# A ninth ring slot in a mixture-of-experts layer, half of the gate's weights loaded before the last expert's, and a loop body moved from expert 2 to expert 28

## The chip, the core and the metric

The kernel runs on one core of a Trainium2 chip. The metric is the device time of one execution in microseconds (us), lower being better. A core has TensorE (PE; its weight loads are listed as PEld), VectorE (DVE), ScalarE (ACT), GpSimd (POOL) and SyncE (SP), which here only issues transfers. The core's 16 DMA engines move data between the device's memory and SBUF, the memory on chip.

## The reference, cut to what matters

One layer on 512 tokens of width 1024: attention and retention with an output projection, then a mixture of 32 experts of which each token goes to four, then a gate on a per-layer embedding.

```python
x = x + concatenate([y_a, y_b]) @ w_out                 # attention, retention
hn = rmsnorm(x); top4 = top_k(hn @ w_router + b_router, 4)
for each expert e, for its tokens:                      # 32 experts, 4 of them a token
    h = hn @ w_up_gate[e] + b_up_gate[e]                # 1024 -> 2048
    y = act(h) @ w_down[e] + b_down[e]                  # 1024 -> 1024
    x[token] += gate * y
gate = sigmoid(rmsnorm(x) @ w_ple_gate)                 # 1024 x 1024
x = x + (p @ w_ple_proj) * gate
```

## The kernel before

Everything up to the router takes the first 350 us. Then a loop written out for e = 0 to 31 runs the experts, one after the other. The products of an expert are made with its weights as the moving operand, so the time on TensorE is that of streaming 12.6 MB of weights through it. An expert with more than 64 tokens does more: under an `If` on its count it computes 32 further rows (`up32`, `act32`, `down32`). These are called wide here, the others narrow.

**The ring.** Weights come in pieces of 2 MB: pieces 0 to 3 of an expert are its up and gate weights, 4 and 5 its down weights. They go into eight slots of `[128, 4096]` floats, `NRING = 8`. `load(n)` issues the n-th piece on SP's queue (a down piece as two transfers of half its size); n counts six pieces an expert, with one more item in front of expert 28 (`AT_P`: the embedding rows p and their projection, which stay in their slot to the end) and the two halves of `w_ple_gate` behind the last expert. `ring_slot` says which slot each takes: that of the piece eight before it. In the loop, `load(6 * e + 8 + c)` stands behind the last use of piece c of expert e: for c = 0 to 3 after `up` and `up32`, for 4 and 5 at the expert's end. SP waits there until TensorE has read the slot.

**The results of an expert** go to `y_d` in the device's memory (`rows_out`, `rows_out32`, issued by POOL). In experts 28 to 31 `fetch_all(k)`, k = 3 down to 0, gathers a row for each of the 512 tokens back, in four transfers of 512 KB into four tiles `gy0` to `gy3`, and `add_y(k, t)` adds each into `acc` on DVE at the end of the expert; those of k = 0 are added behind the loop.

**Blocks beyond 96.** `later_blocks()` handles experts with more than 96 tokens, in a loop `For_i(0, nb)` under `If(nb > 0)`. It is called at the start of expert 2. With these inputs no instruction of its body is in the trace: every engine jumps over it.

**The tail.** With `in_order`, the order of PE, DVE, ACT and POOL is that of the code. `g_scale`, `g_hi` and `g_lo` scale the gate's weights and split them into two parts, a row block k of 8 at a time; blocks 0 to 3 (`K0`) are in the first half of `w_ple_gate`, 4 to 7 (`K1`) in the second. Then `yparts` splits the last expert's result, `join_last(t)` adds it into `acc` on TensorE and DVE, `z_parts` turns `acc`, and `terms` and `gated` make the gate's product.

Of the kernel before, what the change touches and what calls it, by code (L numbers as in the profile page):

```python
# [19 lines left out]
P = 128  # L20
# [25 lines left out]
def f32(ap):  # L46
    return ap.bitcast(F32)
# [3 lines left out]
def layer_kernel(ctx, tc, a, out, dbg=None, stop=None):  # L51
# [116 lines left out]
    order = (4, 3, 0, 5, 6, 1, 2, 7)  # L168

    AT_P = 6 * E - 24
    ring_slot = list(order)
    for n in range(NRING, 6 * E + 3):
        ring_slot.append(ring_slot[n - NRING + (n - NRING >= AT_P)])
# [4 lines left out]
    def loaded(e, c):  # L180
        n = 6 * e + c
        return n + (n >= AT_P)

    def piece(e, c):
        return ring(loaded(e, c)).rearrange("p (k f) -> p k f", k=2 if c < 4 else 4)

    def ple_views():
        t = ring(AT_P)
        return (t[:, 0:2 * D].rearrange("p (k d) -> p k d", k=2),
                t[:, 2 * D:2 * D + NT * PLE].rearrange("p (t d) -> p t d", t=NT),  # L190
                t[:, 3 * D:4 * D].rearrange("p (k t) -> p k t", k=2))

    def load(n, halves=(0, 1)):

        if n == AT_P:
# [3 lines left out]
            return  # L201
        if n in (6 * E + 1, 6 * E + 2):
            nc.sync.dma_start(ring(n).rearrange("p (k f) -> p k f", k=4),
                              w_pg.rearrange("(h k p) f -> h p k f", h=2, p=P)[n - 6 * E - 1])
        e, c = divmod(n - (n > AT_P), 6)
        if e < E:
            v = ring(n)
            if c < 4:
                src = w_up[e].rearrange("(m p c) f -> m p (c f)", m=4, c=2)[c]
                if len(halves) == 2:  # L210
                    nc.sync.dma_start(v, src)
                else:
                    o = slice(halves[0] * 2048, halves[0] * 2048 + 2048)
                    nc.sync.dma_start(v[:, o], src[:, o])
            else:
                v = v.rearrange("p (i f) -> p i f", i=2)
                src = w_dn[e].rearrange("(m i p c) f -> m p i (c f)", m=2, i=2, c=2)[c - 4]
                for i in halves:
                    nc.sync.dma_start(v[:, i, :], src[:, i, :])
# [325 lines left out]
    def by_rows(t):  # L545
        return t.rearrange("p (k f) -> p k f", k=4)
# [428 lines left out]
    def later_blocks():  # L975
# [3 lines left out]
        with tc.If(nb > 0):  # L979
            with tc.For_i(0, nb):  # L980
# [31 lines left out]
                oh = m1.tile([P, S], F32R, name="ooh", tag="gy2")  # L1012
# [8 lines left out]
                def rows_of(src, mul, add, per, i):  # L1021

                    fi = m1.tile([P, 1], F32, name=f"ofi{i}", tag="ofi", bufs=2)
                    ii = m1.tile([P, 1], I32, name=f"oii{i}", tag="oii", bufs=2)
                    nc.vector.tensor_scalar(fi, slot, float(per), float(add), op0=ALU.mult, op1=ALU.add)
                    nc.vector.scalar_tensor_tensor(fi, eid, float(mul), fi, op0=ALU.mult, op1=ALU.add)
                    nc.vector.tensor_copy(ii, fi)
                    w = m1.tile([P, D], F32, name=f"ow{i}", tag=f"gy{i % 2}")
# [18 lines left out]
                yy = m1.tile([P, D], F32R, name="oy", tag="gy3")  # L1047
                for h in range(2):
                    pt = dbank(f"opy{h}")
                    hs = slice(h * 512, (h + 1) * 512)  # L1050
                    for k in range(4):
                        nc.tensor.transpose(pt[0:B, k * P:(k + 1) * P], yTo[:, 4 * h + k, :], ident)
                    nc.scalar.activation(yy[0:B, hs], pt[0:B, :], AF.Copy)
                    nc.vector.tensor_tensor(yy[B:2 * B, hs], pt[0:B, :], f32(yy[0:B, hs]), op=ALU.subtract)
                for t in range(NT):
                    nc.vector.scalar_tensor_tensor(key, gates[:, t, 0, :], 1.0, one, op0=ALU.mult, op1=ALU.mult,
                                                   accum_out=st[:, 2:3])
                    for h in range(2):
                        pc = dbank(f"opc{t}{h}")
                        nc.tensor.matmul(pc, oh[:, t * P:(t + 1) * P], yy[:, h * 512:(h + 1) * 512], start=True, stop=True)  # L1060
# [133 lines left out]

    def join_last32():

        ys = []
        for i, tag in enumerate(("gy0", "gy1")):
            ys.append(m1.tile([P, D], F32R, name=f"yq{i}", tag=tag))
# [200 lines left out]
    with in_order:  # L1400
        K0, K1 = (0, 1, 3, 2), (4, 6, 5, 7)
        g_scale(3)
        g_scale(5)
        g_scale(7)
        for t in range(NT):
            add_y(0, t)
        for k in (0, 1, 3, 2):
            g_hi(k)
            g_lo(k)
        yparts = [m1.tile([P, 512], F32R, name=f"yl{i}", tag=("y", "gl")[i]) for i in range(2)]  # L1410
        nc.scalar.activation(yparts[0], y64, AF.Copy)
        nc.vector.tensor_tensor(yparts[1], y64, f32(yparts[0]), op=ALU.subtract)
# [67 lines left out]
```

## Time and profile before

| | before |
|---|---|
| median of three runs | 1502.23 us (1500.53 to 1503.43) |
| the profiled execution's own time | 1501.09 us |
| its span, first to last instruction | 1499.3 us |
| mean granted clock of TensorE, as a share of the full 2.4 GHz | 0.979 |
| TensorE busy | 1359.1 us (91% of the span) |
| DVE, ACT, POOL busy | 451.9, 293.4, 184.1 us |
| moved by DMA | 474.79 MB, 317 GB/s over the span |

The expert loop lies from 349.6 to 1426 us. In it both TensorE and the DMA engines are nearly always busy, so the share of the whole span says little; what counts is which of the two the other waits for, stretch by stretch.

### The profile page before, as it was taken

The page shows a single profiled execution, that of the slowest core. Times are in us where ns is not written, and L with a number is a line of the kernel's source. Part 1 is how long each engine was busy: PE and PEld are TensorE (multiplying, and loading weights), DVE is VectorE, ACT ScalarE, POOL GpSimd, SP SyncE. Part 2 cuts the span into 40 slices and gives each one's busy share as a digit, 9 for nine tenths or more (in the row PEclk, how much of TensorE's full clock was granted, in tenths as well). Part 3 has the DMA queues.
Part 4 walks back from the last instruction along what each step waited for, and adds up shares of the span by engine and source line. Part 5 has one row for each costly group of instructions (what it writes and reads, how often), then busy time and mean ns, then how long its engine had stood idle before and what let it go on. Part 6 is the DMA issues. An engine that isn't in the chain of part 4 may idle for free. (4 is left out here: it accounts for less than half of the span.)

```text
span 1499.3 us, 21638 instructions
## 1 busy us (share of the span) xinstructions
PE 1359.1 (91%) x8629; PEld 657.3 (44%) x8629; DVE 451.9 (30%) x1033; ACT 293.4 (20%) x564; POOL 184.1 (12%) x268
## 2 busy tenths in 40 slices
PE   8999999997979999999989899879999988989868
PEld 7776775563334334334323333423333333333246
DVE  4657596555111121112211111211111121123353
ACT  5645674341000000000000000000000000101043
POOL 3132000010110110110100011000111100212140
PEclk9999999998999999999999999989999999999989
DMA  7203604265979999999999999999999999999921
GB/s 283 85 29 87 155 2 168 69 250 220 362 316 389 407 391 404 410 414 408 410 395 412 404 408 412 412 409 409 407 388 377 375 414 405 407 405 407 417 89 57
DMA packets 65526, 474.79 MB, mean 317 GB/s; under 512 B 9484, under 2 KB 10032, under 8 KB 32400
## 3 DMA queue, kind: packets, MB, share of 16 engines
q1 hardware_dynamic: 54192, 441.69, 73.9%
q0 software_dynamic: 11200, 31.22, 5.9%
q8 instruction: 96, 1.57, 0.4%
q14 instruction: 38, 0.31, 0.1%
HBM read 454.40 MB, written 18.48 MB: 315 GB/s over the span
## 5 line engine op out<-in xcount | busy, mean ns | idle before, releaser
L1148 PE MATMUL yb<-ring,hT 128*64 128x512 f32 x1024 | 244.5, 610 | 34.9 <-DVE hT L1141 26.6
L1090 PE MATMUL glu<-ring,xT 128*64 128x512 f32 x1024 | 252.8, 610 | 20.9 <-DMA ring<-in_w_up_gate_dram 20.8
L1090 PE MATMUL lin<-ring,xT 128*64 128x512 f32 x1024 | 244.2, 592 | 0.0
L1126 DVE TENSOR_SCALAR gl<-glu 128x512 f32<-128x512 f32 x32 | 22.1, 692 | 511.0 <-PE glu L1090 511.0
L1090 PEld LDWEIGHTS glu<-ring,xT 128*64 128x64 f32 x1024 | 83.0, 140 | 153.3 <-issue 112.0
L1090 PEld LDWEIGHTS lin<-ring,xT 128*64 128x64 f32 x1024 | 84.0, 138 | 138.5 <-issue 136.1
L1148 PEld LDWEIGHTS yb<-ring,hT 128*64 128x64 f32 x1024 | 65.7, 137 | 151.6 <-issue 100.9
L890 POOL DMA_INDIRECT xg<-hn_d,idx x32 | 31.1, 971 | 783.4 <-DVE idx L889 441.8
L1104 PE MATMUL u<-ring,xT 128*32 128x256 f32 x2048 | 113.6, 379 | 0.6 <-issue 0.6
L1127 ACT ACTIVATE sg<-gl 128x512 f32<-128x512 f32 x32 | 20.1, 629 | 431.1 <-DVE gl L1126 425.6
L1104 PEld LDWEIGHTS u<-ring,xT 128*32 128x32 f32 x2048 | 63.2, 110 | 46.6 <-issue 1.0
L1161 PE MATMUL yc<-ring,hv 128*32 128x256 f32 x1024 | 58.6, 381 | 8.3 <-DVE hv L1157 8.3
L1172 ACT COPY y<-yb 128x512 f32<-128x512 f32 x31 | 18.1, 585 | 228.9 <-PE yb L1148 228.9
L907 ACT COPY xT<-px 128x384 f32<-128x384 f32 x64 | 27.7, 482 | 155.7 <-PE px L906 155.6
L1161 PEld LDWEIGHTS yc<-ring,hv 128*32 128x32 f32 x1024 | 31.7, 110 | 31.3 <-DVE hv L1157 12.1
L906 PE MATMUL px<-ident,xg 96*128 96x96 f32 x256 | 29.2, 259 | 14.0 <-PEq L1297 7.3
L1174 POOL DMA_DIRECT2D y_d<-y x62 | 33.7, 548 | 63.8 <-ACTq L1317 34.6
L1168 POOL DMA_DIRECT2D y_d<-yv x64 | 31.6, 500 | 54.7 <-ACT yv L1166 48.6
L906 PEld LDWEIGHTS px<-ident,xg 96*128 96x128 f32 x256 | 23.4, 146 | 33.6 <-issue 26.3
L1386 PE MATMUL o<-gh,z 128*128 128x512 f32 x128 | 37.1, 398 | 0.2 <-ACT z L1343 0.2
L886 DVE SCALAR_TENSOR_TENSOR scr<-rk,slot,iot 96x512 bf16<-96x512 f32 x32 | 23.9, 747 | 41.0 <-PE rk L880 40.9
L1223 DVE SCALAR_TENSOR_TENSOR acc<-gy,gk,acc 128x1024 f32<-128x1024 f32 x16 | 20.4, 1284 | 41.2 <-DMA gy<-y_d,yidx 41.0
(960 smaller groups left out, 1701.2 us busy)
## 6 DMA issues: line engine op xcount, KB each, us to landing
ring<-in_w_up_gate_dram SPq DMA_DIRECT2D x127, 2048.0 KB, 17.8
ring<-in_w_down_dram SPq DMA_DIRECT2D x128, 1024.0 KB, 24.9
ring<-in_w_in_dram SPq DMA_DIRECT2D x12, 1024.0 KB, 6.4
y_d<-y POOLq DMA_DIRECT2D x62, 128.0 KB, 9.6
ring<-in_w_out_dram SPq DMA_DIRECT2D x4, 1024.0 KB, 5.9
ring<-in_w_ple_gate_dram SPq DMA_DIRECT2D x2, 2048.0 KB, 29.8
y_d<-none SPq DMA_DIRECT2D x2, 1984.0 KB, 12.3
ring<-in_x_dram SPq DMA_DIRECT2D x4, 512.0 KB, 5.4
```

The costliest lines, as they stand in the source:

```text
L886: nc.vector.scalar_tensor_tensor(scr[0:n], rk[0:n], slots[0:n], iot[0:n], op0=ALU.is_equal, op1=ALU.mult, accum_out=idf[0:n])
L890: nc.gpsimd.indirect_dma_start(out=xg[0:n], out_offset=None, in_=hn_d, in_offset=bass.IndirectOffsetOnAxis(ap=idx[0:n, :1], axis=0))
L906: nc.tensor.transpose(pv[:, k, :], xg[0:n, (4 * h + k) * P:(4 * h + k + 1) * P], ident[0:n, 0:n])
L907: nc.scalar.copy(xT[:, 4 * h:4 * h + 4, 0:n], pv)
L1090: nc.tensor.matmul(o[two(j)], xTs[e][:, 2 * m + c, 0:64], w[:, c, f:f + 512], start=False, stop=m == 3 and c == 1)
L1104: nc.tensor.matmul(u32[four(q), g * 256:(g + 1) * 256], xTs[e][:, 2 * m + c, 64:C], w[:, c, f:f + 256], start=False, stop=m == 3 and c == ...
L1126: nc.vector.tensor_scalar(gl, glu, LIMIT, None, op0=ALU.min)
L1148: nc.tensor.matmul(y64[two(j)], hT[:, fc, :], w[:, fc % 4, j * 512:(j + 1) * 512], start=fc == 0, stop=fc == KD - 1)
L1161: nc.tensor.matmul(y32[four(q), 0:256], hT[:, fc % 2, fc // 2, :], w[:, fc % 4, q * 256:(q + 1) * 256], start=fc == 0, stop=fc == KD - 1, ...
L1168: nc.gpsimd.dma_start(y_d[e * C + 64:(e + 1) * C, q * 256:(q + 1) * 256], y[four(q)])
L1174: nc.gpsimd.dma_start(y_d[e * C:e * C + 64, j * 512:(j + 1) * 512], y[two(j)])
L1386: nc.tensor.matmul(banks[t, h], (zh, zl, zh)[i][:, k, ts], (g_h, g_h, g_l)[i][k // 4][:, k % 4, hs], start=first, stop=last)
```

## The change

1. A ninth slot, index `NRING`, is allocated in the memory that `gy0` to `gy3` take later (one tag `gy`, one tile of the four together). It is loaded once before the loop, and takes its turn in the ring until expert 28 needs its memory for the fetched rows: the pieces of experts 28 and 29 skip it, and it is not used again.
2. `items` lists what is loaded in order, and the first half of `w_ple_gate` ("g0") now stands in front of expert 31's pieces; the second ("g1") stays last. A line of slots replaces the fixed distance of eight: each slot gets the next item as it comes free, and `load_behind(e, c)` loads what follows piece c of expert e.
3. `later_blocks()` is called at expert 28 rather than 2, since its body uses the memory of the fetched rows.
4. In the tail, `g_hi` and `g_lo` of blocks 0 to 3 stand ahead of `g_scale(5)`, `g_scale(7)` and `add_y(0, t)`.

```diff
+    items = [(e, c) for e in range(E) for c in range(6)]
+    items.insert(items.index((E - 4, 0)), "p")
+    items.insert(items.index((E - 1, 0)), "g0")
+    items.append("g1")
+    ring_slot, follows, line = [], {}, [(i, None) for i in order]
+    for n, it in enumerate(items):
+        i, before_it = line.pop(0)
+        if i == NRING and (it == "p" or it[0] in (E - 4, E - 3)):
+            i, before_it = line.pop(0)
+        ring_slot.append(i)
+        if before_it is not None:
+            follows[before_it] = n
+        if it not in ("p", "g0"):
+            line.append((i, n))
+        if n == NRING - 1:
+            line.insert(0, (NRING, None))
...
+    def load_behind(e, c):
+        if nth[e, c] in follows:
+            load(follows[nth[e, c]])
...
+    fresh(NRING, "ring8", pool=m1, tag="gy")
+    load(NRING)
+
     def fetch_all(k):
+        gy = m1.tile([P, NT, D], F32, name=f"gy{k}", tag="gy")
         for t in range(NT):
-            fetch_y(k, t, m1.tile([P, D], F32, name=f"gy{k}{t}", tag=f"gy{t}"))
+            fetch_y(k, t, gy[:, t, :])
     for e in range(E):
-        if e == 2:
+        if e == E - 4:
             later_blocks()
...
         for c in range(4):
-            load(6 * e + 8 + c)
+            load_behind(e, c)
...
         g_scale(3)
+        for k in (0, 1, 3, 2):
+            g_hi(k)
+            g_lo(k)
         g_scale(5)
         g_scale(7)
         for t in range(NT):
             add_y(0, t)
-        for k in (0, 1, 3, 2):
-            g_hi(k)
-            g_lo(k)
```

The rest of the diff gives the body of `later_blocks` other buffers. The new lines shift the code by 13 to 17 lines.

**SP, ahead of the loop and through expert 0.** A row is a line of the code and what is loaded into which slot; `ring_2236` is slot 4, `ring_2594` slot 3, `ring_2595` slot 0, `ring_2601` slot 5, `ring_2602` slot 6, `ring_3035` to `ring_3037` slots 1, 2 and 7. Before:

```order
L211 DMA ring_3037<-in_w_up_gate_dram 128x4096
L1210 TENSOR_LOAD cnts
L1297 COMPARE_AND_BRANCH
L1297 UNCONDITIONAL_BRANCH x2
L211 DMA ring_2236<-in_w_up_gate_dram 128x4096
L1309 COMPARE_AND_BRANCH
L1309 UNCONDITIONAL_BRANCH x2
L211 DMA ring_2594<-in_w_up_gate_dram 128x4096
L1317 COMPARE_AND_BRANCH
L1317 UNCONDITIONAL_BRANCH x2
L219 DMA ring_2595<-in_w_down_dram 128x2048 x2
```

Now, with `ring_3179` the ninth slot:

```order
L224 DMA ring_3037<-in_w_up_gate_dram 128x4096
L224 DMA ring_3179<-in_w_up_gate_dram 128x4096
L1223 TENSOR_LOAD cnts
L1314 COMPARE_AND_BRANCH
L1314 UNCONDITIONAL_BRANCH x2
L224 DMA ring_2236<-in_w_up_gate_dram 128x4096
L1326 COMPARE_AND_BRANCH
L1326 UNCONDITIONAL_BRANCH x2
L232 DMA ring_2594<-in_w_down_dram 128x2048 x2
L1334 COMPARE_AND_BRANCH
L1334 UNCONDITIONAL_BRANCH x2
L232 DMA ring_2595<-in_w_down_dram 128x2048 x2
```

Piece 2 of expert 1, which waited for slot 4 and so for expert 0's first piece, goes into the new slot ahead of the loop; from there on every slot that comes free takes the piece after the one that it took before.

**SP, the loads that stand in expert 30's stretch and the last one.** Before:

```order
L211 DMA ring_3036<-in_w_up_gate_dram 128x4096
L211 DMA ring_3037<-in_w_up_gate_dram 128x4096
L1309 COMPARE_AND_BRANCH
L1309 UNCONDITIONAL_BRANCH x2
L1317 COMPARE_AND_BRANCH
L1317 UNCONDITIONAL_BRANCH x2
L211 DMA ring_2594<-in_w_up_gate_dram 128x4096
L219 DMA ring_2595<-in_w_down_dram 128x2048 x2
L219 DMA ring_2601<-in_w_down_dram 128x2048 x2
L203 DMA ring_2602<-in_w_ple_gate_dram 128x4x1024
```

Now:

```order
L216 DMA ring_2601<-in_w_ple_gate_dram 128x4x1024
L1326 COMPARE_AND_BRANCH
L1326 UNCONDITIONAL_BRANCH x2
L1334 COMPARE_AND_BRANCH
L1334 UNCONDITIONAL_BRANCH x2
L224 DMA ring_2602<-in_w_up_gate_dram 128x4096
L224 DMA ring_3035<-in_w_up_gate_dram 128x4096
L224 DMA ring_3037<-in_w_up_gate_dram 128x4096
L224 DMA ring_2236<-in_w_up_gate_dram 128x4096
L232 DMA ring_2594<-in_w_down_dram 128x2048 x2
```

The first half of the gate's weights stood behind all six pieces of expert 31 and stands ahead of them now; each of the six comes one place later.

**DVE, from the last expert's second `hT` copy (L1141, now L1154) to the split of its result (L1412, now L1429).** `gl` is what `g_lo` writes, `acc<-gy` is `add_y`. Before:

```order
L1141 COPY hT_11201<-ph31b 128x2x2x64
L1309 COMPARE_AND_BRANCH
...
L1309 UNCONDITIONAL_BRANCH x2
L1223 SCALAR_TENSOR_TENSOR acc<-gy_11186,gk,acc 128x1024
L1223 SCALAR_TENSOR_TENSOR acc<-gy_11188,gk,acc 128x1024
L1223 SCALAR_TENSOR_TENSOR acc<-gy_11190,gk,acc 128x1024
L1223 SCALAR_TENSOR_TENSOR acc<-gy_11192,gk,acc 128x1024
L1365 SCALAR_TENSOR_TENSOR gl_11364<-ring_2602,pcol,gh_11362 128x1024 x3
L1412 TENSOR_TENSOR yl_11383<-yb_11197,yl_11382 128x512
```

Now:

```order
L1154 COPY hT_11168<-ph31b 128x2x2x64
L1326 COMPARE_AND_BRANCH
...
L1326 UNCONDITIONAL_BRANCH x2
L1382 SCALAR_TENSOR_TENSOR gl_11331<-ring_2601,pcol,gh_11329 128x1024 x3
L1236 SCALAR_TENSOR_TENSOR acc<-gy_11156,gk,acc 128x1024 x4
L1429 TENSOR_TENSOR yl_11350<-yb_11164,yl_11349 128x512
```

The three `g_lo` have changed places with the four `add_y`.

## Rows read from the trace of the kernel before

**Rows 1.** The page's 40 slices of 37.5 us: GB/s that the DMA engines moved.

```profile
GB/s 283 85 29 87 155 2 168 69 250 220 362 316 389 407 391 404 410 414 408 410 395 412 404 408 412 412 409 409 407 388 377 375 414 405 407 405 407 417 89 57
```

**Rows 2.** Stretches: us, busy time by engine, granted clock, DMA share, GB/s.

```profile
360.00:371.50 11.50, 11.41 (x109) 4.64 (x113) 4.22 (x9) 0.63 (x1) 0.00 (x0) 1.00 0.12 27
...
440.00:452.00 12.00, 11.30 (x58) 4.80 (x54) 2.80 (x6) 1.49 (x3) 0.00 (x0) 1.00 0.21 64
...
560.00:1098.00 538.00, 489.17 (x3437) 193.93 (x3434) 89.42 (x216) 40.18 (x81) 49.84 (x83) 0.99 1.01 408
...
1098.00:1185.00 87.00, 81.64 (x680) 31.99 (x678) 16.86 (x40) 7.21 (x15) 8.01 (x14) 1.00 0.95 379
...
425.00:434.00 9.00, 2.67 (x50) 1.48 (x40) 0.00 (x0) 0.37 (x1) 1.98 (x4) 0.83 1.05 391
```

**Rows 3.** TensorE in order of time: starts of experts 2, 23, 24 and 25.

```profile
433.73 0.67 PE L1084 MATMUL glu<-bst,bsel 96*64 96x512 bf16 x2 [6.33 <-PEq L979]
...
1127.33 0.41 PE L1084 MATMUL glu<-bst,bsel 96*64 96x512 bf16 x2
...
1164.23 0.41 PE L1084 MATMUL glu<-bst,bsel 96*64 96x512 bf16 x2
...
1190.34 0.43 PE L1084 MATMUL glu<-bst,bsel 96*64 96x512 bf16 x2 [0.53 <-PEq L1317]
```

**Rows 4.** TensorE in order of time: waits for weights, experts 13, 20, 29 and 31.

```profile
786.09 3.50 PE L1090 MATMUL glu<-ring,xT 128*64 128x512 f32 x8 [3.47 <-DMA ring<-in_w_up_gate_dram]
...
1027.33 1.94 PE L1090 MATMUL glu<-ring,xT 128*64 128x512 f32 x8 [1.16 <-DMA ring<-in_w_up_gate_dram]
...
1335.41 3.62 PE L1090 MATMUL glu<-ring,xT 128*64 128x512 f32 x8 [2.79 <-DMA ring<-in_w_up_gate_dram]
...
1409.30 1.94 PE L1090 MATMUL glu<-ring,xT 128*64 128x512 f32 x8 [1.14 <-DMA ring<-in_w_up_gate_dram]
```

**Rows 5.** Granted clock and TensorE's work after two idle stretches, same columns as rows 2.

```profile
430.90:437.70 6.80, 3.97 (x12) 1.87 (x14) 0.00 (x0) 0.00 (x0) 0.00 (x0) 0.50 1.04 429
...
1438.90:1444.60 5.70, 4.96 (x18) 3.19 (x19) 3.12 (x5) 1.19 (x2) 4.90 (x2) 0.50 0.00 0
```

**Rows 6.** Ahead of the loop: DVE's last work on the router's tiles; SP's first issue in the loop.

```profile
357.34 0.25 DVE L824 SCALAR_TENSOR_TENSOR hit<-vts,mv,gz 128x31 f32<-128x31 f32 x1
...
369.74 2.06 SPq L211 DMA_DIRECT2D ring<-in_w_up_gate_dram  x2
```

**Rows 7.** TensorE's starts of experts 28 to 31; SP's first issue behind expert 28's up weights.

```profile
1285.90 0.41 PE L1084 MATMUL glu<-bst,bsel 96*64 96x512 bf16 x2
1317.61 0.43 PE L1084 MATMUL glu<-bst,bsel 96*64 96x512 bf16 x2 [0.55 <-PEq L1317]
...
1364.11 0.41 PE L1084 MATMUL glu<-bst,bsel 96*64 96x512 bf16 x2
...
1393.42 0.43 PE L1084 MATMUL glu<-bst,bsel 96*64 96x512 bf16 x2 [0.54 <-PEq L1317]
...
1305.98 1.58 SPq L211 DMA_DIRECT2D ring<-in_w_up_gate_dram  x3
```

**Rows 8.** The tail in order of time, DVE, TensorE and ACT.

```profile
1420.59 0.42 DVE L1141 COPY hT<-ph31b 128x256 f32<-128x256 f32 x1 [3.88 <-PE ph31b L1140]
1421.07 5.37 PE L1148 MATMUL yb<-ring,hT 128*64 128x512 f32 x24 [0.52 <-DVEq L1309]
...
1430.67 1.28 DVE L1223 SCALAR_TENSOR_TENSOR acc<-gy,gk,acc 128x1024 f32<-128x1024 f32 x1 [1.43 <-DMA gy<-y_d,yidx]
1431.37 2.19 ACT L1355 ACTIVATE gh<-ring,pcol 128x1024 fp32r<-128x1024 f32 x2 [18.68 <-DMA ring<-in_w_ple_gate_dram]
1432.56 2.64 DVE L1365 SCALAR_TENSOR_TENSOR gl<-ring,pcol,gh 128x1024 fp32r<-128x1024 f32 x2 [0.61 <-ACT gh L1355]
1438.03 0.68 DVE L1412 TENSOR_TENSOR yl<-yb,yl 128x512 fp32r<-128x512 f32 x1
1438.92 1.31 PE L1187 MATMUL pc<-yl,oh 64*128 64x512 f32 x4 [12.48 <-DVEq L1413]
```

More of the change, by code (lines that the diff above doesn't have):

```diff
@@ L168, in layer_kernel @@
     order = (4, 3, 0, 5, 6, 1, 2, 7)
[L172 to L175, printed above, removed]
+    items = [(e, c) for e in range(E) for c in range(6)]
+    items.insert(items.index((E - 4, 0)), "p")
+    items.insert(items.index((E - 1, 0)), "g0")
+    items.append("g1")
+    nth = {it: n for n, it in enumerate(items)}
+    ring_slot, follows, line = [], {}, [(i, None) for i in order]
[10 more added lines that the diff above has]
+            line.insert(0, (NRING, None))
     def ring(n):
         return slots[ring_slot[n]]
-    def loaded(e, c):
-        n = 6 * e + c
-        return n + (n >= AT_P)
     def piece(e, c):
-        return ring(loaded(e, c)).rearrange("p (k f) -> p k f", k=2 if c < 4 else 4)
+        return ring(nth[e, c]).rearrange("p (k f) -> p k f", k=2 if c < 4 else 4)
+    def load_behind(e, c):
+        if nth[e, c] in follows:
+            load(follows[nth[e, c]])
     def ple_views():
-        t = ring(AT_P)
+        t = ring(nth["p"])
         return (t[:, 0:2 * D].rearrange("p (k d) -> p k d", k=2),
@@ L200, in load @@
             nc.sync.dma_start(wpp, w_pp.rearrange("(k p) d -> p k d", p=P))
[L201 to L202 removed]
+        elif items[n] in ("g0", "g1"):
             nc.sync.dma_start(ring(n).rearrange("p (k f) -> p k f", k=4),
[L204 to L206 removed]
+                              w_pg.rearrange("(h k p) f -> h p k f", h=2, p=P)[int(items[n][1])])
+        else:
+            e, c = items[n]
             v = ring(n)
@@ L1011, in later_blocks @@
                 nc.tensor.matmul(rk, esel, rankT, start=True, stop=True)
-                oh = m1.tile([P, S], F32R, name="ooh", tag="gy2")
+                big = m1.tile([P, 4, D], F32, name="obig", tag="gy")
+                oh = m1.tile([P, S], F32R, name="ooh", tag="y")
                 nc.vector.tensor_scalar(oh, rk, sl, None, op0=ALU.is_equal)
@@ L1027, in rows_of @@
                     nc.vector.tensor_copy(ii, fi)
-                    w = m1.tile([P, D], F32, name=f"ow{i}", tag=f"gy{i % 2}")
+                    w = big[:, i % 4, :]
                     nc.gpsimd.indirect_dma_start(out=w, out_offset=None, in_=src,
@@ L1046, in later_blocks @@
                     nc.scalar.copy(yTo[:, 4 * i:4 * i + 4, :], chunks(yTb[i], B))
-                yy = m1.tile([P, D], F32R, name="oy", tag="gy3")
+                yy = [m1.tile([P, 512], F32R, name=f"oy{h}", tag=("h", "sg")[h]) for h in range(2)]
                 for h in range(2):
                     pt = dbank(f"opy{h}")
-                    hs = slice(h * 512, (h + 1) * 512)
                     for k in range(4):
                         nc.tensor.transpose(pt[0:B, k * P:(k + 1) * P], yTo[:, 4 * h + k, :], ident)
-                    nc.scalar.activation(yy[0:B, hs], pt[0:B, :], AF.Copy)
-                    nc.vector.tensor_tensor(yy[B:2 * B, hs], pt[0:B, :], f32(yy[0:B, hs]), op=ALU.subtract)
+                    nc.scalar.activation(yy[h][0:B], pt[0:B, :], AF.Copy)
+                    nc.vector.tensor_tensor(yy[h][B:2 * B], pt[0:B, :], f32(yy[h][0:B]), op=ALU.subtract)
                 for t in range(NT):
@@ L1059, in later_blocks @@
                         pc = dbank(f"opc{t}{h}")
-                        nc.tensor.matmul(pc, oh[:, t * P:(t + 1) * P], yy[:, h * 512:(h + 1) * 512], start=True, stop=True)
+                        nc.tensor.matmul(pc, oh[:, t * P:(t + 1) * P], yy[h], start=True, stop=True)
                         o = acc[:, t, h * 512:(h + 1) * 512]
@@ L1195, in join_last32 @@
     def join_last32():
-        ys = []
-        for i, tag in enumerate(("gy0", "gy1")):
-            ys.append(m1.tile([P, D], F32R, name=f"yq{i}", tag=tag))
+        yq = m1.tile([P, 2, D], F32R, name="yq", tag="gy")
+        ys = [yq[:, i, :] for i in range(2)]
+        for i in range(2):
             nc.vector.tensor_scalar(ys[i].rearrange("p (a f) -> p a f", f=512), oh, 0.0, None, op0=ALU.mult)
@@ L1320, in layer_kernel @@
         for c in range(4, 6):
-            load(6 * e + 8 + c)
+            load_behind(e, c)
         if k < TOPK:
@@ L1324, in layer_kernel @@
                 add_y(k, t)
-    w_g = [by_rows(ring(6 * E + 1 + i)) for i in range(2)]
-    used = [ring_slot[n] for n in (loaded(E - 1, 4), loaded(E - 1, 5), 6 * E + 1, 6 * E + 2, AT_P)]
+    w_g = [by_rows(ring(nth[f"g{i}"])) for i in range(2)]
+    used = [ring_slot[n] for n in (nth[E - 1, 4], nth[E - 1, 5], nth["g0"], nth["g1"], nth["p"])]
     free = [i for i in range(NRING) if i not in used]
```

2 lines of the change are left out of this document (1 added, 1 removed).

## The prediction

> **What bounds the kernel now.** I read the slices first. From the sixteenth on (562 us) nearly every one moves 404 to 417 GB/s [rows 1], and over 560 to 1098 us the DMA share is 1.01 [rows 2]: the engines are full. TensorE is busy nine tenths of the same time, so both look like the bound, and the waits have to decide. In the list of what TensorE waited for, the stops for weights lie in two stretches, experts 12 to 20 and 27 to 31; four of them are in [rows 4]. An expert that waits for nothing takes 26.1 us when narrow (1164.23 to 1190.34) and 36.9 us when wide (1127.33 to 1164.23) [rows 3]. The stream needs, per piece: from the wait at 786.09 (expert 13, piece 1) to that at 1027.33 (expert 20, piece 3) 44 pieces came in 241.2 us, 5.48 us each with all other transfers, or 32.9 us an expert [rows 4]. About half of the experts are wide, so TensorE would need 31.5 us on average: the stream is the slower of the two, and the ring only decides how much of the stream's time is lost before it becomes the bound. From 1335.41 (expert 29, piece 3) to 1409.30 (expert 31, piece 3) it is 12 pieces in 73.9 us, 6.16 us each, since gathered rows share the engines [rows 4].
>
> So what I price is **idle time of the DMA engines inside the loop**; it moves the end one for one, as long as TensorE still catches up with the stream afterwards. There are three such stretches of size. Share 0.12 over 11.5 us after 360: 10.1 us. Share 0.21 over 12 us after 440: 9.5 us. Share 0.95 against 1.01 over 87 us after 1098 (the three wide experts 21 to 23, where TensorE is slower and the ring is full): 5.2 us [rows 2].
>
> **The tail** is read from the end of the chain of waits, which is TensorE from 1438.92 on. It had finished the last expert at 1426.4 (1421.07 + 5.37) and then sat 12.48 us [rows 8]. What it waited for is a sequence on DVE: the last `add_y` begins at 1430.67, `g_lo` from 1432.56 waits for ACT's `g_hi`, which waited 18.68 us for the gate's weights until 1431.37, and the split of the result (`yl`) is done at 1438.7 [rows 8].
>
> **The change, part by part.**
>
> *Jump moved away from expert 2.* Experts 1 and 2 should meet without a gap, but TensorE sits 6.33 us at the branch over the body, L979 [rows 3], and then works 3.97 us at half clock [rows 5], which loses 2.0: 8.3 us. At that point no weights are waited for, so on TensorE alone this would be absorbed later. But the loads behind expert 2 are issued only when it has used its pieces, and meanwhile the engines run dry: 9.5 us after 440. With TensorE 8.3 us earlier the idle shrinks by 8.3. **-8.3 us** for everything behind it.
>
> *Ninth slot, ahead of the loop.* Its load waits for what used that memory; DVE's last work on the router's tiles ends at 357.6, and SP's first issue in the loop is at 369.74 [rows 6], after which transfers start at about 371.5. The idle stretch has 10.1 us of room, and a piece of 2.1 MB takes 5.0 us even at 417 GB/s [rows 1], so it fits. From there each release of a slot issues the piece after the one it issued before: the stream is one piece ahead at the same instant and its later idle is the same. Where TensorE waits for it (experts 12 to 20) a piece is worth 5.48 us. **-5.5 us**; the lower bound is 0, if the lead were lost before expert 12. Here the Trainium skill (page "DMA: Bandwidth & Descriptors", section Specifications) gives about 358 GB/s as a core's share of the memory; by that an estimate of a piece is 5.9 us. The rows' 408 GB/s over 538 us go beyond it, so the measurement decides, and the sum would differ by 0.4.
>
> *Ninth slot, again at experts 21 to 24.* Behind expert 20 both TensorE and the stream are 13.8 us early. In the 5.2 us of idle that follow the ring is full; one more slot lets the stream go on for up to one piece of 5.0 us. **-5.0 us** (bounds 0 and 5.2).
>
> *Slot retired, jump at expert 28.* From expert 26 on the ring is eight slots again, and TensorE now loses the 8.3 us ahead of expert 28. Where is it then? Expert 24 starts at 1164.23 - 13.8 = 1150.4; three narrow and a wide expert (78.3 + 36.9), 1 us of waits and the jump give 1274.9 for expert 28, against 1285.90 [rows 7]. Its first issue comes 20.1 us after its start (1305.98 - 1285.90), at 1295.0. Had the stream run through, expert 29's piece 0, the last one issued by then, would land at 1335.41 less three pieces (18.5) less 18.8, at 1298.1. So the queue holds 3 us at that moment, which about covers the time from issue to first bytes. Between 0 and 6 us of idle (6 if the jump costs twice as much), I take **+2 us**. The stream is then 16.8 us early.
>
> The jump bears on a rule that speaks against this part: the Trainium skill (page "Runtime: NRT & Kernel Launch", section Instruction fetch mechanics) says that a taken branch to code outside the window forces a DMA fetch of the target before work goes on. At expert 2 the share was 1.05 while TensorE sat there [rows 2], so the 6.33 us were already paid with full engines; I keep the price.
>
> *First half of the gate ahead of expert 31.* Each of its six pieces lands one place later, 6.16 us; the lower bound is 5.0, a bare piece. Piece 3 is used at 1409.30 - 16.8 + 6.2 = 1398.7, 10.6 us earlier than before. TensorE is there in time: from 1274.9 on, experts 28 to 30 take 31.7, 42.0 (46.5 less the wait of 2.79 and 1.7 of half clock) and 29.3 us [rows 4, 7], so expert 31 starts at 1377.9.
>
> *Tail.* The `hT` copy that ended at 1421.0 ends at 1410.4, and TensorE ends at 1415.8. `g_hi` is done by then, so DVE goes on with three `g_lo` (1.32 each, two of them are the 2.64 [rows 8]) to 1414.4, four `add_y` (1.28 each) to 1419.5, and `yl` to 1420.2; TensorE goes on at **1420.4**, 18.5 us earlier. The last row to be added began at 1430.67, 37.3 us after expert 30's end (1393.42); from 1377.9 that is 1415.2, before DVE comes to it. The second half of the gate lands with the end of the stream, about 1416, 20 us before its products.
>
> *Clock.* Before, 4.96 us of TensorE's work behind 1438.90 ran at half clock [rows 5], losing 2.5 us. The stop is now 4.6 us instead of 12.5; behind the 3.47 us stop at 786.09 eight products still took 3.50 us instead of 1.94 [rows 4]. I take **-1 us** of the possible 2.5.
>
> *Free:* reading four rows into one tile makes the first gather of an expert wait for all four additions of the one before. They would end 2 us before the gather's other wait, the landing of the rows just written. If that cover went, each us would go into `add_y` of k = 0, which has 4 us of slack.
>
> **Sum:** -18.5 - 1.0 = -19.5 us on the profiled execution's 1501.09, 1481.6; that execution is 1.1 us under the median of the three, so I say **1482 us** for the median.
>
> **Rivals.**
>
> *Queue dry at expert 28.* For it: 3 us of queue, and a slot fewer. If the idle were 8.3, the whole of the jump, the stream is 10.5 early: 1488. Against: the work above.
>
> *More gain.* No idle at 28, a place in the queue worth 5.0, no half clock behind the tail: 2 + 1.2 + 1.5 more, 1477.
>
> *The lead is worth nothing* because slots come free late anyhow, and only the jump's 8.3 less 2 counts: piece 3 of expert 31 is used at 1409.2, the tail starts 8.0 early: 1493. Against: the engines' idle is plain in the rows.
>
> *Slower.* The jump at expert 28 stalls TensorE much longer than at expert 2. Each us beyond the 8.3 and the 3 in the queue is idle of the stream. It ends slower than before only when the stop at expert 28 passes 6.3 + 21.5 = 28 us; at 32 us the time is 1506. The rows show no stop at a branch over 6.33. (The Trainium skill's page on the runtime, named above, sets no bound to such a fetch.)
>
> *No change:* gains by the lead lost, and the gate's place (+6.2) paid with nothing but the tail's order to win: piece 3 at 1409.30 + 6.2, minus 8.3 and plus 8.3 for the jump, start of the tail at 1437.3: 1500.
>
> **Chances.** My forecast 0.62 (its own range 1478 to 1487), queue dry 0.14, more gain 0.10, lead worthless 0.05, no change 0.04, slower 0.05. The range that leaves out no more than 2 in 10 goes from 1475 to 1491. 0.2% (3 us) is about what this kernel's measurement can tell; faster by more has 0.91, within it 0.04, slower 0.05.
>
> **What would show it.** Right: no gap of 6 us ahead of expert 2 and one ahead of expert 28; a DMA share near 1 instead of 0.95 over the wide experts 21 to 23; waits for weights among experts 12 to 20 later and fewer; expert 31 waiting for its up weights by 2 us or more; TensorE's stop before `pc` about 5 us instead of 12.5. Wrong: a DMA share well under 1 between 1270 and 1320; a stop at expert 28 beyond 8 us; `add_y` of k = 0 waiting for its rows.

## The result, and the profile after

The changed kernel takes **1485.93 us** (median of 4 runs, 1485.12 to 1488.94) against 1502.26 before: a ratio of 0.9896, 95% interval 0.9881 to 0.9911. The profiled execution takes 1485.39 us with a span of 1483.5, so from profile to profile it is 15.7 us faster where 19.5 were forecast. Lines have moved by 13 to 17: L1097 is the start of an expert (L1084 before), L1103 its up products, L992 the branch over the later blocks' body, L1236 `add_y`, L1382 `g_lo`, L1200 `pc`.

Stretches of the changed kernel: us, busy time by engine, granted clock, DMA share, GB/s. The first four answer to those of [rows 2], the fourth 14 us earlier, since TensorE is that much ahead; the last two lie around expert 28's first issue.

```profile
360.00:371.50 11.50, 11.50 (x113) 4.65 (x117) 4.05 (x8) 0.63 (x1) 0.00 (x0) 1.00 0.56 215
425.00:434.00 9.00, 9.00 (x78) 3.44 (x70) 0.00 (x0) 0.37 (x1) 1.98 (x4) 1.00 1.01 360
440.00:452.00 12.00, 10.32 (x51) 3.58 (x49) 4.41 (x11) 1.49 (x3) 0.96 (x1) 1.00 0.88 341
...
1084.00:1171.00 87.00, 80.44 (x670) 31.68 (x668) 16.54 (x39) 7.31 (x15) 8.02 (x14) 0.98 0.97 392
1270.00:1320.00 50.00, 40.15 (x209) 15.55 (x203) 9.49 (x15) 4.91 (x11) 7.87 (x11) 0.93 0.91 350
...
1292.00:1298.00 6.00, 6.00 (x23) 2.15 (x23) 0.00 (x0) 1.17 (x2) 0.00 (x0) 1.00 0.91 366
1298.00:1304.00 6.00, 5.09 (x28) 1.90 (x24) 3.03 (x7) 1.49 (x3) 0.00 (x0) 1.00 0.32 73
```

The hole at 440 has all but closed (share 0.21 to 0.88) and that at 360 by about half (0.12 to 0.56: about the one piece more), and TensorE works through 425 to 434 where it sat. A new hole has opened at 1298: with 1.01 as full, 0.6 + 4.1 us of idle in the two slices, about 5 us with the next one (0.97 over 1304 to 1310).

TensorE in order of time, and SP's first issue behind expert 28's up weights, changed kernel (start, length, work, and in brackets the stop ahead of it and what ended it): the starts of experts 21, 28 and 31, two stops inside experts 24 and 26, and expert 31's waits.

```profile
1039.21 0.41 PE L1097 MATMUL glu<-bst,bsel 96*64 96x512 bf16 x2
...
1166.62 1.35 PE L919 MATMUL px<-ident,xg 96*128 96x96 f32 x8 [2.35 <-PEq L1314]
...
1222.44 0.85 PE L919 MATMUL px<-ident,xg 96*128 96x96 f32 x8 [1.48 <-DVE h L1147]
...
1279.65 0.67 PE L1097 MATMUL glu<-bst,bsel 96*64 96x512 bf16 x2 [7.17 <-PEq L992]
...
1301.95 1.56 SPq L224 DMA_DIRECT2D ring<-in_w_up_gate_dram  x3
...
1383.60 0.43 PE L1097 MATMUL glu<-bst,bsel 96*64 96x512 bf16 x2 [0.54 <-PEq L1334]
...
1386.82 1.94 PE L1103 MATMUL glu<-ring,xT 128*64 128x512 f32 x8 [2.57 <-DMA ring<-in_w_up_gate_dram]
1392.45 1.94 PE L1103 MATMUL glu<-ring,xT 128*64 128x512 f32 x8 [1.97 <-DMA ring<-in_w_up_gate_dram]
```

Expert 28 starts at 1279.65, 6.25 us earlier than in [rows 7], and SP issues the first load behind its up weights at 1301.95, not at the 1295.0 of the forecast. That is where the new hole comes from.

The tail of the changed kernel in order of time, VectorE, TensorE and ACT, which answers to [rows 8].

```profile
1412.98 0.42 DVE L1154 COPY hT<-ph31b 128x256 f32<-128x256 f32 x1 [2.40 <-PE ph31b L1153]
1413.83 3.68 DVE L1382 SCALAR_TENSOR_TENSOR gl<-ring,pcol,gh 128x1024 fp32r<-128x1024 f32 x3 [0.42 <-DVEq L1326]
1417.42 4.87 DVE L1236 SCALAR_TENSOR_TENSOR acc<-gy,gk,acc 128x1024 f32<-128x1024 f32 x4
1422.20 0.69 DVE L1429 TENSOR_TENSOR yl<-yb,yl 128x512 fp32r<-128x512 f32 x1
...
1413.46 5.68 PE L1161 MATMUL yb<-ring,hT 128*64 128x512 f32 x24 [0.52 <-DVEq L1326]
1423.09 1.31 PE L1200 MATMUL pc<-yl,oh 64*128 64x512 f32 x4 [3.95 <-DVEq L1430]
...
1407.01 2.19 ACT L1372 ACTIVATE gh<-ring,pcol 128x1024 fp32r<-128x1024 f32 x2 [0.40 <-PEq L1314]
```

VectorE goes from the copy to the split of the result without a wait, in the order forecast; TensorE's stop is 3.95 us instead of 12.48, and the tail starts at 1423.09 instead of 1420.4.

### The profile page after: what moved, and what is told of

Read it like the earlier page. It is cut to its first block, busy times and chain, and to the rows that moved or that the text cites. A ratio compares the mean times of both kernels' runs of the same rounds, so it can differ in the third digit from the quotient of the medians.

```text
span 1483.5 us, 21634 instructions
## 1 busy us (share of the span) xinstructions
PE 1353.6 (91%) x8629; PEld 652.0 (44%) x8629; DVE 451.4 (30%) x1033; ACT 293.3 (20%) x564; POOL 182.4 (12%) x268
## 5 line engine op out<-in xcount | busy, mean ns | idle before, releaser
L1103 PE MATMUL glu<-ring,xT 128*64 128x512 f32 x1024 | 247.6, 599 | 16.3 <-DMA ring<-in_w_up_gate_dram 16.3
L1103 PE MATMUL lin<-ring,xT 128*64 128x512 f32 x1024 | 245.5, 594 | 0.0
L1103 PEld LDWEIGHTS glu<-ring,xT 128*64 128x64 f32 x1024 | 81.9, 138 | 145.5 <-issue 115.8
L1103 PEld LDWEIGHTS lin<-ring,xT 128*64 128x64 f32 x1024 | 83.0, 137 | 139.5 <-issue 139.5
L903 POOL DMA_INDIRECT xg<-hn_d,idx x32 | 30.5, 954 | 781.3 <-DVE idx L902 469.0
L1140 ACT ACTIVATE sg<-gl 128x512 f32<-128x512 f32 x32 | 20.1, 629 | 408.8 <-DVE gl L1139 408.8
L1141 DVE TENSOR_TENSOR gl<-gl,sg 128x512 f32<-128x512 f32 x32 | 22.2, 692 | 24.4 <-ACT sg L1140 23.7
```

The lines of the kernel that those rows point to most:

```text
L903: nc.gpsimd.indirect_dma_start(out=xg[0:n], out_offset=None, in_=hn_d, in_offset=bass.IndirectOffsetOnAxis(ap=idx[0:n, :1], axis=0))
L1103: nc.tensor.matmul(o[two(j)], xTs[e][:, 2 * m + c, 0:64], w[:, c, f:f + 512], start=False, stop=m == 3 and c == 1)
L1141: nc.vector.tensor_tensor(gl, gl, sg, op=ALU.mult)
```

## The experiments

My theory (A): the end follows the stream of weights; the body's place at expert 2 and the ninth slot ahead of the loop are worth their full price, but at expert 28 TensorE comes late, the DMA queue runs dry for about 5 us and hands most of the lead of experts 21 to 24 back. The rivals: the jump costs the same wherever it stands; the slot's lead is worth nothing; the gate's place, not the stream, made the gain.

Each ratio is to the kernel before on the same chip (1502.49 us for the first four runs, 1500.68 for the next four, 1500.97 for the last four).

| run | median us | ratio to before, 95% interval |
|---|---|---|
| e1_jump28_alone | 1495.58 | 0.996, 0.9947 to 0.9973 |
| e2_after_nojump | 1481.51 | 0.9858, 0.9844 to 0.9872 |
| e3_before_nojump | 1494.93 | 0.9949, 0.9936 to 0.9962 |
| e4_jump31 | 1493.76 | 0.9948, 0.9936 to 0.9961 |
| e5_eight_slots | 1494.27 | 0.9956, 0.9943 to 0.997 |
| e6_slot_till_20 | 1486.74 | 0.9903, 0.9888 to 0.9918 |
| e7_gate_last | 1487.84 | 0.9915, 0.9901 to 0.9928 |
| e8_old_tail | 1486.98 | 0.991, 0.9895 to 0.9925 |
| e9_jump13 | 1480.75 | 0.9866, 0.9851 to 0.9881 |
| e10_jump13_lo_later | 1477.89 | 0.9846, 0.9832 to 0.9859 |
| e11_lo_later | 1485.77 | 0.9905, 0.989 to 0.992 |
| e12_ones_early | 1477.27 | 0.9842, 0.9828 to 0.9855 |

**The body's place** (four runs). The kernel before with the body moved:

```diff
-        if e == 2:
+        if e == E - 4:
             later_blocks()
```

> The kernel before with one edit: the later blocks' body stands ahead of expert 28 instead of expert 2. Theory A (the jump at expert 2 held the stream of weights up, at expert 28 the queue of eight slots hides it): the stream is 8.3 us earlier behind expert 2. Expert 29's piece 0, due about 1316.9 in the kernel before, would come at 1308.6, after the first issue behind the jump (1305.98 - 8.3 + 7.2 = 1304.9), so nothing is given back: 1502.2 - 8.3 = 1494 us. Theory B (the jump costs the same wherever it stands): 1502 us. Theory C (the DMA queue runs dry at expert 28 in this kernel too): 1497 to 1499 us.

The kernel before without the call:

```diff
-        if e == 2:
-            later_blocks()
```

> The kernel before without the later blocks' body; it leaves out the tokens of an expert beyond 96, of which these inputs have none. Theory A (the jump at expert 2, its 6.33 us and 2 us of half clock, puts the stream back one for one): 1502.2 - 8.3 = 1494 us, and as long as with the body at expert 28. Theory B (the ring takes the jump in, since the stream is the bound later): 1502 us.

The changed kernel without it (`if e == E - 4: later_blocks()` taken out):

> The changed kernel without the later blocks' body, so without its jump; it leaves out the tokens of an expert beyond 96, of which these inputs have none. Theory A (the 7.17 us jump ahead of expert 28 lets the DMA queue run dry for about 5 us, and the end follows the stream): expert 28 starts 7.2 us earlier, its first issue comes at about 1294.8, before expert 29's piece 0 lands (1296.24), the stop of the stream at 1292 to 1302 is gone, and the time is 1486 - 5 = 1481 us. Theory B (the jump is hidden at expert 28): 1486 us. Theory C (all 7.2 us of it are on the path): 1479 us or less.

Before gains 7.6 us without the body (1502.49 to 1494.93) and 6.9 us with it at expert 28; the two intervals overlap, so in that kernel expert 28 hides the jump but for 0 to 2 us. The changed kernel gains 4.4 us without it by medians, 5.7 by the ratios. Theory A holds in the second and third of these runs; in the first, 1495.58 lies between A's 1494 and C's 1497, and its trace has about 1 us of idle (share 0.82 over 1306 to 1312). The slice at 1298 of the changed kernel without the jump, and SP's first issue there:

```profile
1298.00:1304.00 6.00, 4.63 (x26) 1.92 (x27) 2.32 (x7) 0.86 (x2) 0.00 (x0) 1.00 0.97 364
...
1297.70 1.61 SPq L224 DMA_DIRECT2D ring<-in_w_up_gate_dram  x3
```

The issue comes 4.25 us earlier, not the 7.2 expected, because experts 24 and 26 took 31.80 and 31.78 us in this execution (30.54 and 28.91 in the changed kernel's). Even so the share is 0.97 instead of 0.32: the hole is gone. My reading is that the ninth slot had used up what hid the jump: a stream further ahead has less left in the queue when TensorE is late.

The body ahead of expert 31 (`if e == E - 1`, its tiles `both` and `w` in `big`):

> The changed kernel with the later blocks' body ahead of expert 31 instead of expert 28 (two of its tiles, which nothing uses when it does not run, lie in its own buffer so that it can stand there). Theory A (at expert 28 the jump stops the stream for about 5 us; ahead of expert 31 all loads but one are issued, and TensorE waits 2.57 and 1.97 us for expert 31's weights anyway): the stream is 5 us earlier, the jump takes the place of these two waits, 1486 - 4.5 = 1481.5 us. Theory B (the jump costs the same wherever it stands): 1486 us. Theory C (at the end of the loop it is added to what TensorE waits for): 1488 us or more.

Theory A missed: at 1493.76 the body costs more here, as theory C had it. The trace of this run, VectorE and TensorE in order of time around the branch:

```profile
1368.36 5.37 PE L1161 MATMUL yb<-ring,hT 128*64 128x512 f32 x24 [0.52 <-DVEq L1326]
...
1376.24 1.28 DVE L1236 SCALAR_TENSOR_TENSOR acc<-gy,gk,acc 128x1024 f32<-128x1024 f32 x1 [4.87 <-DMA gy<-y_d,yidx]
1382.39 1.28 DVE L1236 SCALAR_TENSOR_TENSOR acc<-gy,gk,acc 128x1024 f32<-128x1024 f32 x1 [4.87 <-DMA gy<-y_d,yidx]
1388.65 0.67 PE L1097 MATMUL glu<-bst,bsel 96*64 96x512 bf16 x2 [14.91 <-DVEq L992]
```

TensorE was done at 1373.73 and stood 14.91 us, not 7. VectorE waited for fetched rows twice and ended at 1383.67; TensorE went on 4.98 us later, and the profile names VectorE as what ended its stop. So the stop at the branch contains a wait for VectorE here, which I had priced at nothing, and its additions (L1236) make it long. That the hole at 1298 is gone here too (share 1.01 over 1266 to 1320) did not pay for it.

**The ninth slot** (two runs). The changed kernel with eight slots:

```diff
-        if n == NRING - 1:
-            line.insert(0, (NRING, None))
...
-    fresh(NRING, "ring8", pool=m1, tag="gy")
-    load(NRING)
```

> The changed kernel without the ninth slot: eight slots throughout, the rows' buffer stands by until expert 28; all else as changed. Theory A (a piece of lead ahead of the loop is kept to the end, and the gate's first half ahead of expert 31 pays because the tail no longer waits for it): TensorE's start of the tail comes 8 us behind a last expert that its piece 3 (1402.21 + 6.2 us by the run with only the body moved) holds up for about 4 us, at 1427.4 against 1423.09: 1490 to 1491 us. Theory B (the lead is lost before the end): 1486 us. Theory C (ninth slot worth all of 5.5 + 5.0 us): 1496 us.

1494.27 us: the slot is worth 8.3 us by medians and 9.0 by the ratios, between theories A and C. The traces say where: expert 21 starts 5.9 us later with eight slots (1045.11 against 1039.21), expert 31's first weights are used 7.3 us later (1394.08 against 1386.82), and the tail starts 8.8 us later (1431.85 against 1423.09). The last step is not the stream's: the eight products behind that first wait took 3.58 us with eight slots and 1.94 with nine.

The slot given up behind expert 20:

```diff
-        if i == NRING and (it == "p" or it[0] in (E - 4, E - 3)):
+        if i == NRING and (it == "p" or it[0] in range(21, E - 2)):
```

> The changed kernel with the ninth slot given up behind expert 20 instead of behind expert 25, all else as changed. Theory A (the slot lets the stream run on at experts 21 to 24 by 2 to 2.5 us, but at expert 28 the stream then runs dry for 5 us because TensorE comes late, so this lead is given back there): the same as the changed kernel, 1486 us. Theory B (a lead of 2.5 us kept to the end): 1488 us. Theory C (the 5.0 us of the forecast): 1491 us. In either case the DMA share over 1084 to 1171 us falls from 0.97 to 0.94.

1486.74, the same as the changed kernel within the intervals. Its two stretches, which answer to 0.97 and 0.91 above:

```profile
1084.00:1171.00 87.00, 80.33 (x668) 31.15 (x663) 16.60 (x40) 7.22 (x15) 8.02 (x14) 0.98 0.92 371
1270.00:1320.00 50.00, 40.10 (x217) 15.67 (x211) 9.49 (x15) 4.91 (x11) 8.27 (x12) 0.93 0.98 385
```

With 1.01 as full, the idle is 7.8 + 1.5 = 9.3 us here and 3.5 + 5.0 = 8.5 in the changed kernel. So by one profile of each the slot did earn 4.3 us at experts 21 to 24, near the 5.0 of the forecast, and 3.5 of them were given back at expert 28. The issues agree: the first load behind expert 28 goes out at 1302.24 here and at 1301.95 there, and expert 31's first weights are used at 1386.65 and 1386.82.

**The gate and the tail** (two runs). The gate's edit undone whole, and the tail's order alone undone:

```diff
-    items.insert(items.index((E - 1, 0)), "g0")
-    items.append("g1")
+    items += ["g0", "g1"]
```

```diff
         g_scale(3)
-        for k in (0, 1, 3, 2):
-            g_hi(k)
-            g_lo(k)
         g_scale(5)
         g_scale(7)
         for t in range(NT):
             add_y(0, t)
+        for k in (0, 1, 3, 2):
+            g_hi(k)
+            g_lo(k)
```

The first run has both edits, the second only the lower one.

> The changed kernel with both halves of the gate's weights behind expert 31 and the tail in its old order, so without the edit on the gate. Theory A (expert 31's pieces come 6.2 us earlier, which saves TensorE its 4.5 us of waits, but the first half of the gate lands at 1417.2 instead of 1381.9, and the split of the result ends 8.0 us behind that, as in the run with only the body moved): TensorE starts the tail at 1425.4 instead of 1423.09, 1488 us. Theory B (the gate's place is all that matters in the tail, 12 us of stop as in the kernel before): 1494 us. Theory C (nothing but the waits for expert 31's weights counts): 1481 us.

> The changed kernel with the tail's old order on VectorE and GpSimd (the four additions first, then the high and low parts of the gate), the gate's first half still loaded ahead of expert 31. Theory A (VectorE has 3.68 us of low parts and 4.87 us of additions in front of the split of the result in either order, and nothing in them waits): 1486 us, the same within 1 us. Theory B (the order is what pays: the additions wait for their rows, or the low part on GpSimd stands behind the scaling that waits for the second half until 1423.66 and holds TensorE up): 1488 to 1491 us.

1487.84 and 1486.98. Against 0.9896 the gate's edit is worth 0.0019 or 2.9 us by the ratios and 1.9 by the medians, but the two intervals overlap (0.9901 to 0.9928 and 0.9881 to 0.9911), so the times alone do not show it; the order alone shows no difference that its interval tells from none either. In the first of the two, TensorE and VectorE at the start of the tail:

```profile
1424.30 0.68 DVE L1428 TENSOR_TENSOR yl<-yb,yl 128x512 fp32r<-128x512 f32 x1
1425.18 1.31 PE L1199 MATMUL pc<-yl,oh 64*128 64x512 f32 x4 [10.79 <-DVEq L1429]
```

TensorE stands 10.79 us, near the 12.48 of [rows 8], and starts at 1425.18 where 1425.4 was expected: a stop of 3.95 instead of 10.79 buys 2.1 us, because the pieces of expert 31 pay for it. In the run with eight slots the gate's edit bought nothing that can be seen (0.9956 against the 0.996 of the body's move alone).

**A better place for the body, and the tail** (four runs). The body ahead of expert 13, with its weight rows in a tile of its own (two more of its tiles change buffers):

```diff
-        if e == E - 4:
+        if e == 13:
             later_blocks()
...
-                    w = big[:, i % 4, :]
+                    w = ringC.tile([P, D], F32, name=f"ow{i}", tag="bd3")
```

> The changed kernel with the later blocks' body ahead of expert 13, and with its fetched weight rows in a small tile of their own instead of the ninth slot's memory, so that it can stand there; the body does not run with these inputs. Theory A (TensorE waits about 10 us for weights among experts 13 to 20 anyway, which takes the jump in; expert 12 is narrow, so GpSimd's last issue before the branch comes earlier than ahead of expert 28, and TensorE stands 4.5 to 5 us instead of 7.2): from expert 21 on as the kernel without the jump, 1481.5 us, and the waits for weights of experts 13 to 20 are shorter by 4 to 6 us in sum. Theory B (the jump costs the same wherever it stands): 1486 us. Theory C (the loads behind the jump come late and the stream has a gap there): 1483 to 1488 us.

1480.75: theory A. TensorE's waits in experts 13 to 20, first the changed kernel, then this one (what waited, us in total, times, longest):

```profile
PE glu L1103 <- DMA ring<-in_w_up_gate_dram: 11.7, 8, 2.5
```

```profile
PE glu L1095 <- PEq L992: 8.4, 1, 8.4
...
PE glu L1101 <- DMA ring<-in_w_up_gate_dram: 1.6, 2, 1.3
```

The 8.4 us at the branch took the place of 10.1 us of waits for weights, where 4 to 6 were expected. The length of the stop was missed too: 8.42 us, not 4.5 to 5, though the expert ahead is narrow.

Then the three low parts on VectorE behind the first tile's transposes, with the body at 13 and at 28, and at last the one-hot tiles earlier:

```diff
         for k in (0, 1, 3, 2):
             g_hi(k)
-            g_lo(k)
+        g_lo(3)
...
         z_parts(0)
+        for k in (0, 1, 2):
+            g_lo(k)
```

> As the kernel with the body ahead of expert 13, and three of the gate's four low parts (the three on VectorE) behind the first tile's transposes instead of ahead of the additions. Theory A (they are 3.68 us in the sequence that ends with the split of the result, and their products come 7 us later): TensorE's stop ahead of the tail falls by up to 3.7 us to below 1 us, and 1481.5 - 3 = 1478.5 us. Theory B (another work sets the tail's start, or the low parts hold the second tile's addition up by as much): 1481.5 us.

> The changed kernel with only the three low parts of the gate on VectorE moved behind the first tile's transposes; the body stays at expert 28. Theory A (VectorE's 3.68 us of low parts are on the path from the last copy of hT to the split of the result): 1486 - 3 = 1483 us, TensorE's stop ahead of the tail 3.95 - 3.7 us, so below 1 us. Theory B (the delay comes back at the second tile, whose addition stands behind them): 1486 us.

```diff
+        if e == E - 1:
+            oh = ones_last()
         up(e, 2)
...
-        if e == E - 1:
-            oh = ones_last()
         for c in range(4):
```

> As the kernel with the body ahead of expert 13 and the low parts moved, and the two one-hot tiles of expert 31 (1.48 us on VectorE, between the gate of the products and the first copy of hT) made two pieces earlier, where VectorE idles. Theory A (they hold the first copy of hT up by 1.4 us, and TensorE behind it): 1478.5 - 1.4 = 1477 us. Theory B (TensorE has slack there): 1478.5 us.

With the body at 13 the move of the low parts brings 2.9 us (1480.75 to 1477.89; by the ratios 3.0, with intervals that overlap a little); the stop ahead of the tail is 1.62 us, not below 1. With the body at 28 the run is inconclusive: its executions go from 1480.40 to 1488.48, and the median is that of the changed kernel. The profiled one is the fastest of them, and its stretch at expert 28 shows no dry queue, where the changed kernel's profile has 0.91:

```profile
1270.00:1320.00 50.00, 42.31 (x175) 16.02 (x177) 9.50 (x15) 5.13 (x11) 6.59 (x9) 0.93 0.99 392
```

This execution has the jump at expert 28 as well, and the reason that the queue does not run dry can be read from it. Expert 24 as a stretch, first the changed kernel's and then this one's; this one's stop inside it, its start of expert 28, and SP's first issue there:

```profile
1149.91:1180.45 30.54, 26.62 (x117) 8.86 (x114) 4.66 (x11) 2.40 (x5) 2.93 (x5) 0.89 0.94 380
...
1148.85:1176.76 27.91, 23.90 (x118) 8.06 (x114) 4.66 (x11) 2.30 (x5) 2.93 (x5) 1.00 0.94 380
...
1165.36 0.85 PE L919 MATMUL px<-ident,xg 96*128 96x96 f32 x8 [2.15 <-DVE h L1147]
...
1274.65 0.67 PE L1097 MATMUL glu<-bst,bsel 96*64 96x512 bf16 x2 [6.71 <-PEq L992]
...
1297.20 1.58 SPq L224 DMA_DIRECT2D ring<-in_w_up_gate_dram  x3
```

TensorE stops 2.15 us inside expert 24, nearly as long as the 2.35 of the changed kernel, but goes on at full clock; expert 26 takes 27.53 us instead of 28.91. So expert 28 starts 5.0 us earlier, and the issue comes 4.75 us earlier. The dry queue of the changed kernel's profile thus needs both the jump and the half clock behind the stops inside experts 24 and 26: without either one the hole is nearly gone. With both it is there in the profiles of the gate's two runs as well (0.92 and 0.91 over 1270 to 1320). That this also makes the spread of the times is likely but not shown, as there is one profile of each kernel; with the body at 13 the executions lie within 0.94 us of each other in one kernel (1480.26 to 1481.20) and within 4.48 in the next (1475.89 to 1480.37). The one-hot tiles bring 0.6 us, which the intervals do not tell from nothing. In the last kernel, VectorE and TensorE at the start of the tail, and expert 31's first wait:

```profile
1383.39 1.12 PE L1101 MATMUL glu<-ring,xT 128*64 128x512 f32 x2 [7.33 <-DMA ring<-in_w_up_gate_dram]
...
1413.13 1.94 PE L1159 MATMUL yb<-ring,hT 128*64 128x512 f32 x8 [0.96 <-DMA ring<-in_w_down_dram]
1416.68 0.83 PE L1198 MATMUL pc<-yl,oh 64*128 64x512 f32 x4 [1.62 <-DVEq L1428]
...
1408.61 5.31 DVE L1234 SCALAR_TENSOR_TENSOR acc<-gy,gk,acc 128x1024 f32<-128x1024 f32 x4 [0.16 <-DVEq L1324]
1415.79 0.69 DVE L1427 TENSOR_TENSOR yl<-yb,yl 128x512 fp32r<-128x512 f32 x1 [1.87 <-ACTq L1428]
```

TensorE now meets the stream itself: it waits 7.33 us for expert 31's first piece and 0.96 us for its last, which would explain that the one-hot tiles bring so little. At 0.9842 (0.9828 to 0.9855) this kernel is faster than the one before and than the changed one (0.9896, 0.9881 to 0.9911).

## Why the prediction was right, step by step

*What bounds it.* Right: taking the jump away ahead of expert 28 closed a hole of the DMA engines of about 5 us and moved the end by 4.4 to 5.7.

*Jump moved, -8.3.* Right: -7.6 us (5.7 to 9.6 by the interval) where only the call was taken out, -6.9 where it moved to 28. The mechanism shows in the share of 0.88 at 440.

*Ninth slot ahead of the loop, -5.5.* Right: expert 21 starts at 1039.21, and at 1053.5 before (1164.23 of [rows 3] less three experts of 36.9), 14.3 us earlier; 13.8 were forecast for this and the jump together. In the two kernels with the jump moved and eight slots it starts at 1043.90 and 1045.11, so the slot's part is 4.7 to 5.9 us.

*Ninth slot at experts 21 to 24, -5.0.* Right in mechanism (4.3 us against eight slots there), but the sum counted it to the end.

*Slot retired and jump at expert 28, +2.* This is the step that failed in size: about 5 us of idle (4.4 to 5.7 by the run without the jump). Its bounds of 0 to 6 held it. I had SP's first issue behind expert 28 at 1295.0 and it came at 1301.95. From 1149.9, where expert 24 starts, to 1279.65 are 129.7 us, against 115.2 for three narrow and one wide expert; the other 14.5 are the 7.17 of the jump, 2.35 and 1.48 of stops inside experts 24 and 26, and the last 3.5, by difference, the half clock behind these two stops. I had allowed 9.3 in all. Expert 28 then took 22.3 us to its first issue instead of 20.1, at half clock behind the jump. The half clock stands in these stretches of the changed kernel:

```profile
1166.81:1173.64 6.83, 6.13 (x20) 2.20 (x18) 0.57 (x2) 0.96 (x2) 0.00 (x0) 0.50 0.94 363
1224.84:1228.25 3.41, 3.41 (x10) 0.78 (x6) 0.00 (x0) 0.00 (x0) 0.00 (x0) 0.50 1.01 428
1276.04:1282.87 6.83, 3.22 (x10) 1.56 (x12) 0.00 (x0) 0.00 (x0) 0.00 (x0) 0.50 1.00 407
```

I took experts with no wait for weights to need their bare time; a stop that no weight causes costs as much. The trace of the kernel before had such a stop: its expert 25 is narrow and took 28.67 us, at a granted clock of 0.82 from 1204 to 1212. Why TensorE stops 2.35 us behind expert 24's skipped branch (L1314) was not tried. Of the rivals, the dry queue had the place right and the size (8.3) too large; its 1488 is nearer to the measured 1485.93 than my 1482, and its sign, a DMA share well under 1 between 1270 and 1320, came: 0.91.

*Gate ahead of expert 31, +6.2, and the tail.* Right in order, and no addition waited for its rows. Expert 31's piece 3 is used at 1403.2 (1398.7 forecast, and the waits are at pieces 0 and 1), the copy ends at 1413.40 (1410.4), the tail starts at 1423.09 (1420.4). So the stream is 4.5 us late at piece 3, and only 2.7 of it are left at the tail: the other 1.8 are luck. From piece 3 to the copy's end I took the 11.7 us of the kernel before, of which a stretch ran at half clock; the changed kernel took 10.2 us. VectorE then took 9.7 us instead of 10.0. The stretch, in the kernel before:

```profile
1417.34:1420.75 3.41, 3.21 (x10) 0.59 (x6) 0.16 (x1) 0.00 (x0) 0.72 (x1) 0.50 1.01 407
```

The net gain of the gate's edit is 1438.92 - 1437.3 = 1.6 us by the sum of the rival "no change"; measured were 1.9 to 2.9, by runs whose intervals overlap.

*Clock, -1.* Wrong where I put it: behind the stop nothing came back. The tail of the changed kernel still starts at half clock behind a stop of 3.95 us:

```profile
1422.81:1429.64 6.83, 5.83 (x20) 3.88 (x21) 4.06 (x7) 1.19 (x2) 5.67 (x2) 0.50 0.00 1
```

5.83 us of work there lose 2.9, before it was 4.96 and 2.5 [rows 5]. The 2.7 and the 1 are 3.7 of the 3.8 us by which the forecast was too fast.

*The stop at the branch.* Forecast 6.33 again, measured 7.17, under the 8 that would have spoken against me. The Trainium skill (page "Runtime: NRT & Kernel Launch", section Instruction fetch mechanics) says that a taken branch out of the prefetched window waits for a fetch of its target. The traces agree that there is a stop at each place (6.33, 7.17, 8.42 us), but the 14.91 us ahead of expert 31 are for the larger part a wait for VectorE. In the others TensorE goes on 3.58 us (before), 4.43 us (changed) and 6.37 us (body at 13) after GpSimd's last issue; how they divide into a fetch and a wait for another engine stays open.

## What to carry to other kernels

Idle time of a full DMA stream is only won if no later place gives it back: after a lead has been won, look for the next point where the engine that frees the buffers is late, and compare its first issue with the end of the queue there. A lead in the stream and a stop of the computing engine draw on the same queue, so the price of a stop is not its own property: the same jump cost 0 to 2 us at expert 28 with eight slots and 4.4 to 5.7 with nine, and with nine it left hardly a hole in an execution in which TensorE came 5 us earlier. A stop that cannot be removed belongs where the computing engine waits for the stream anyway and the other engines have nothing open.

## What the runs showed of the hardware

- TensorE's stop at a branch over a body can contain a wait for another engine: ahead of expert 31 it stood 14.91 us and went on 4.98 us after VectorE's last addition, 14.92 us after its own last product, and the profile names VectorE as what ended the stop.
- A stop of TensorE of 2.35 us inside expert 24 was followed by 6.83 us at a granted clock of 0.50, the lower level of 1.2 GHz: expert 24, narrow, took 30.5 us (1149.9 to 1180.5) instead of 26.1, 2.35 of it the stop and 2.1 behind it. At the same place in another run a stop of 2.15 us was followed by full clock, and the expert took 27.9 us. So even a short stop can cost more than its length, and the same code can pay this in one execution and not in the next.
